# A Mamba gated RMS norm by one matmul on all partitions, with ln, exp and a Newton step, and a new schedule of the steps around it

## The chip, the cores and the metric

The kernel runs on one core of a Trainium2 chip. The metric is the device time of one execution in microseconds; the median of several runs counts. A core has five engines with queues of their own that synchronise by semaphores: PE (TensorE: matmuls, with its weight loads shown as PEld), DVE (VectorE), ACT (ScalarE), POOL (GpSimd) and SP (SyncE, here the issuer of most DMAs).

## The reference

A decoder trunk of two layers over 256 tokens of width 2048: a Mamba-2 mixer, then a block-sparse attention, each followed by a gated convolutional FFN and a post-norm. The change lies in the Mamba mixer alone:

```python
zxbcdt = x @ w_in
z, xbc, dt = ...
xbc = silu(causal_dwconv(xbc, conv_w, conv_b))
dt = softplus(dt + dt_bias)
a = -exp(a_log)
y = ssd_chunked(xs * dt[..., None], a * dt, b_ssm, c_ssm)
y = y + d_skip[:, None] * xs
y = y.reshape(Bsz, S, D_INNER) * silu(z)
yg = y.reshape(Bsz, S, N_SSM_GROUPS, D_INNER // N_SSM_GROUPS)
yg = yg * rsqrt(mean(square(yg), axis=-1, keepdims=True) + RMS_EPS)
y = yg.reshape(Bsz, S, D_INNER) * norm_w
return y @ w_out
```

There are 8 groups of 512 channels (8 heads of 64). The scan works in two chunks of 128 tokens; it needs the decays exp(acum[l] - acum[s]) within a chunk and exp(acum[l]) for the state that enters the second chunk. Everything is float32.

## The kernel before

All matrix products with weights run in split precision: a weight tile (128 partitions by 1024, 512 KB) is loaded by SP into `raw`, ScalarE makes its high part `hi` (L190), VectorE the low part `lo = raw - hi` (L191), and PE multiplies both with the split activations. One weight tile is one *step*. The body of the kernel is one loop over all steps: `products(i)` issues the matmuls of step i, and in the middle of a step `splits(i)` issues the split of the tile that is three steps ahead (four `hi` and four `lo` buffers, so a split has to wait until PE is done with the tile four before). After a step, `run(post, i)` issues whatever `at(i, f, ...)` has put there. So the order of each engine's queue is written out by hand, by step numbers; each engine works its queue strictly in that order, and dependences across engines become semaphore waits.

In the Mamba part, the columns of `w_in` for B, C and dt come first. Then follow the eight groups, each with eight steps of its x columns (`chX[g]`) and eight of its z columns (`chZ[g]`); `s0` is the first step of a group, so s0+16 is the next group's s0. In these steps the weights stand in PE and the activations stream. An even step multiplies first the high parts (L247: eight products with 512 columns) and then the low parts (L250: eight with 256 columns); an odd step the low parts first. The high products of an odd and the next even step thus stand side by side, and likewise the low ones.

Around these steps the group's own work is spread:

- `m_load` (s0+3): two POOL DMAs bring the cumulated decays of 8 heads, repeated over all partitions, into `mA` (one per chunk, two buffers).
- `m_decay` (s0+6 and s0+7, L717): eight ScalarE activations a chunk, `mA = relu(aux - mA)`; `m_exp` (s0+8, s0+9, L728): `exp(-mA)`.
- `m_into` (s0+7, L724): exponentials of the raw `mA` of the second chunk into `eA`, before its decays overwrite it.
- `m_cb` (s0+7): three PE products of B and C (L703, L704) into a PSUM tile, the masked `cb` by VectorE (L706) and a copy `bc` by ScalarE (L710).
- `Conv.gather` (L581, L582) and `Conv.taps` (ScalarE L604, VectorE L609) at s0+4 and s0+5 for one half of x, at s0+8 and s0+9 for the other; then Silu (L739), the masks (L732), transposes of `xc` (L748) into `xdt`, and the skip `y_d` (L757).
- after the z columns (next group's first steps): `y_off` and `y_diag` (PE L774, L765), then `z_gate` (s0+20), `z_square` (s0+21), `z_sum` (s0+22).
- `z_rms` (s0+23, L804): two PE products with one column each turn the sums of 128 partitions into one mean per token, tokens on partitions; VectorE adds epsilon (L806), POOL raises to the power -0.5 (L807).
- `z_diag` (s0+24, L813): two diagonals of these values. `z_scale` (s0+29, that is the next group's s0+13): a PE product of `ones` with the diagonals (L818) spreads them over all partitions, and VectorE scales `y` (L821). `z_split` (s0+30): the high and low part of `y` (L827, L828) for the output product. The last group's two run at s0+26 and s0+27, in the output projection.

PSUM tiles of these small products come from `tp_tile()` (two buffers); `xdt`, `y` and `sz` from four buffers of `t4k`.

Of the kernel before, what the change touches and what calls it, by code (L numbers as in the profile page):

```python
# [18 lines left out]
F32 = mybir.dt.float32  # L19
F32R = mybir.dt.float32r  # L20
AF = mybir.ActivationFunctionType
OP = mybir.AluOpType
AX = mybir.AxisListType

P = 128
D = 2048
S = 256
# [3 lines left out]
NG = 8  # L31
# [7 lines left out]
RMS_EPS = 1e-5  # L39
# [3 lines left out]
LINE = 64  # L43
# [48 lines left out]
def yoco_kernel(ctx: ExitStack, tc: tile.TileContext, x, lmg, lmb, lfg, lfb, x_t, columns, w, out):  # L92
    nc = tc.nc
    base = ctx.enter_context(tc.tile_pool(name="base", bufs=1))
# [12 lines left out]
    def tp_tile():  # L107
        return psum.tile([P, NC], F32, tag="tp", name="tp", bufs=2)


    ident = base.tile([P, P], F32, name="ident")
# [8 lines left out]
    def c1(name, j):  # L120
        i = COL_AT[name] + j
        return cols[:, i:i + 1]
# [201 lines left out]
    def at(i, f, *a):  # L324
        post.setdefault(i, []).append((f, a))
# [16 lines left out]
    bufs = {"h": base.tile([P, KD, 2, S], F32R, name="hT")}  # L342
# [146 lines left out]
    mhalf = base.tile([P, 2, 1], F32, name="mhalf")  # L489
# [32 lines left out]
    def open_pool(name):  # L522
        g = tc.tile_pool(name=name, bufs=1)
        pool[name] = (g, g.__enter__())
        return pool[name][1]
# [24 lines left out]
    ps = tp_tile()  # L550
# [7 lines left out]
    for p in range(2, 8):  # L558
# [3 lines left out]
    mp = open_pool("mamba")  # L562
# [4 lines left out]
    nc.gpsimd.memset(tri, 1.0)  # L567
    nc.gpsimd.affine_select(out=tri, in_=tri, compare_op=OP.is_ge, fill=0.0, base=0, pattern=[[1, P]],
                            channel_multiplier=-1)
    mean = base.tile([P, LINE], F32, name="mean")  # L570
    nc.gpsimd.memset(mean, 1.0 / NC)
    ones = base.tile([P, P], F32, name="ones")
    nc.gpsimd.memset(ones, 1.0)
    acum_d = dram.tile([NH, S], F32, name="acum_d")
    aux = mp.tile([P, 5, NH], F32, name="aux")

# [45 lines left out]
    def conv4(ch, j, dst, jd):  # L622

        return Conv(ch, j, dst, jd, [k * 48 for k in range(4)], "cw", "cb")
# [58 lines left out]
    G = [dict() for _ in range(NG)]  # L683
# [15 lines left out]
    def m_cb(g):  # L699
        ps = tp_tile()  # L700
        for c in range(2):
            sl = slice(c * P, (c + 1) * P)
            nc.tensor.matmul(ps[:, sl], BT[:, g, sl], CT[:, g, sl], start=True, stop=True)  # L703
        nc.tensor.matmul(ps[:, 2 * P:3 * P], BT[:, g, :P], CT[:, g, P:], start=True, stop=True)  # L704
        cb = mp.tile([P, 2, P], F32, tag="cb", name="cb", bufs=1)
        nc.vector.tensor_mul(cb, ps[:, :2 * P].rearrange("p (c l) -> p c l", c=2),  # L706
                             tri.unsqueeze(1).to_broadcast([P, 2, P]))

        bc = mp.tile([P, P], F32, tag="bc", name="bc", bufs=1)
        nc.scalar.copy(bc, ps[:, 2 * P:3 * P])  # L710
        G[g]["cb"], G[g]["bc"] = cb, bc

    def m_decay(g, c):

# [2 lines left out]
            nc.scalar.activation(t[:, h, :], t[:, h, :], AF.Relu, scale=-1.0, bias=aux[:, 2 + c, 8 * g + h:8 * g + h + 1])  # L717

    def m_into(g):

        G[g]["eA"] = e = mp.tile([P, 4, P], F32, tag="eA", name="eA", bufs=1)
        for q in range(2):
            ps = slice(64 * q, 64 * q + 64)
            nc.scalar.activation(e[ps], G[g]["A", 1][ps].rearrange("p (j q) l -> p j q l", q=2)[:, :, q, :], AF.Exp)  # L724

    def m_exp(g, c):
        t = G[g]["A", c]
# [6 lines left out]
    def x_new(g):  # L734
        G[g]["xc"] = mp.tile([P, 4, S], F32, tag="xc", name="xc")
        return G[g]["xc"]
# [62 lines left out]

    def z_rms(g):  # L800

        ps = tp_tile()
        for h in range(2):
            nc.tensor.matmul(ps[:, h:h + 1], G[g]["sz"][:, 0, h * P:(h + 1) * P], mean[:, :1], start=True, stop=True)  # L804
        rr = mp.tile([P, 2, 1], F32, tag="rr", name="rr")
        nc.vector.tensor_scalar(rr[:, :, 0], ps[:, :2], RMS_EPS, None, op0=OP.add)  # L806
        nc.gpsimd.tensor_tensor(rr, rr, mhalf, op=OP.pow)  # L807
        G[g]["rr"] = rr

    def z_diag(g):  # L810
        G[g]["rd"] = rd = mp.tile([P, 2, P], F32, tag="rd", name="rd", bufs=1)
        for h in range(2):
            nc.vector.tensor_scalar(rd[:, h], ident, G[g]["rr"][:, h, :], None, op0=OP.mult)  # L813

    def z_scale(g):

        ps = tp_tile()
        nc.tensor.matmul(ps[:, :S], ones, G[g]["rd"].rearrange("p h t -> p (h t)"), start=True, stop=True)  # L818
        y = G[g]["y"]
        for i in range(4):  # L820
            nc.vector.scalar_tensor_tensor(y[:, i, :], y[:, i, :], c1("nw", 4 * g + i), ps[:, :S], op0=OP.mult,  # L821
                                           op1=OP.mult)

    def z_split(g):
        y = G[g]["y"]
# [11 lines left out]
    for g in range(NG):  # L837
        s0 = chX[g].first
        at(s0 + 3, m_load, g)
        at(s0 + 7, m_cb, g)  # L840
        at(s0 + 7, m_into, g)
        at(s0 + 6, m_decay, g, 0)
        at(s0 + 7, m_decay, g, 1)
        at(s0 + 8, m_exp, g, 0)
        at(s0 + 9, m_exp, g, 1)
        conv4(chX[g], 4 * g, lambda g=g: x_new(g), 0).plan()
        at(s0 + 11, x_silu, g)
        at(s0 + 11, m_mask, g, 0)
        at(s0 + 12, m_mask, g, 1)
        if g:  # L850
            at(s0 + 13, z_scale, g - 1)
            at(s0 + 14, z_split, g - 1)
        at(s0 + 13, x_turn, g)
        at(s0 + 13, y_d, g)
        for b in range(2):
            at(chZ[g].ready(b), z_gather, g, b)
            at(chZ[g].ready(b) + 1, z_silu, g, b)
        at(s0 + 18, y_off, g)
        at(s0 + 18, y_diag, g)
        at(s0 + 20, z_gate, g)  # L860
        at(s0 + 21, z_square, g)
        at(s0 + 22, z_sum, g)
        at(s0 + 23, z_rms, g)
        at(s0 + 24, z_diag, g)
    at(s0 + 26, z_scale, NG - 1)
    at(s0 + 27, z_split, NG - 1)


    def chain(norm, nxt=None, after=None):
# [133 lines left out]
    A = {}  # L1003
# [76 lines left out]
    for h in range(HEADS):  # L1080
        i, j = divmod(h, 4)
# [87 lines left out]
```

## Time and profile before

| what | us |
|---|---|
| median of 3 runs (2553.05 to 2553.3) | 2553.09 |
| the profiled execution's own time | 2553.77 |
| its span, first to last instruction | 2552.0 |
| PE busy in the span | 2534.4 |
| VectorE busy | 1648.0 |
| ScalarE busy | 1351.8 |
| POOL busy | 71.7 |

A timeline row has the start in us from the span's beginning, its length, the engine, the line of the kernel, operation, what is written and read, shapes and the count of instructions merged into it; in brackets the idle time before it and what ended that. Lengths overlap: neighbours in one queue are pipelined, so the distance between two starts is the better price. A group row ends with busy us and mean ns of one, then the idle us before them. A float32 matmul that is not in split form appears as two or more records.

### The profile page before, as it was taken

Reading aid. Unit: us, or ns where it says so; the run is one execution under the profiler, and the core shown is the slowest. Engines: PE = TensorE matmul, PEld = TensorE weight load, DVE = VectorE, ACT = ScalarE, POOL = GpSimd, SP = SyncE. Lnnn points to the kernel's source line nnn. Section 1 sums busy time; section 2 is a strip of 40 time slices with the busy share of each in tenths; the row PEclk is TensorE's granted clock in tenths of the full one; section 3 lists DMA queues with packets and bytes.
Section 4 is the critical chain, followed back from the end, with each engine's and each line's share of the span. In section 5 each row is a group of like instructions: output and inputs, shape, how many; then the busy total and the mean of one; then the engine's idle time right before and its main releaser. Section 6 shows DMA issues by size and latency. Waiting matters only on the chain.

```text
span 2552.0 us, 36102 instructions
## 1 busy us (share of the span) xinstructions
PE 2534.4 (99%) x14031; PEld 2202.9 (86%) x14031; DVE 1648.0 (65%) x2122; ACT 1351.8 (53%) x1761; POOL 71.7 (3%) x89
## 2 busy tenths in 40 slices
PE   9999999999999999999999999999999999999998
PEld 8888888888888888888888888888888888888887
DVE  6768777854676766666444645655767666665545
ACT  6677677733455555555334444543555555554333
POOL 0000000000200000000000200000200000000001
PEclk9999999999999999999999999999999999999999
DMA  7655655557565555655666655456655555556564
GB/s 257 204 168 190 199 190 173 190 198 234 184 225 190 184 196 182 198 185 195 202 226 201 221 189 174 158 172 229 217 192 191 189 190 189 185 195 205 198 223 165
DMA packets 141499, 501.02 MB, mean 196 GB/s; under 512 B 15616, under 2 KB 16128, under 8 KB 141328
## 3 DMA queue, kind: packets, MB, share of 16 engines
q1 hardware_dynamic: 136976, 483.45, 57.3%
q0 software_dynamic: 4064, 14.75, 1.7%
q8 instruction: 110, 1.80, 0.3%
q14 instruction: 61, 0.50, 0.1%
q10 hardware_dynamic: 288, 0.52, 0.1%
HBM read 490.20 MB, written 8.45 MB: 195 GB/s over the span
## 4 chain that ended last, share of the span: by engine, by line
PE 93%; ACT 3%; DVE 2%; issue 1%; DMA 0%; SPq 0%; DVEq 0%; ACTq 0%
PE acc L247 37%; PE acc L250 20%; PE acc L218 11%; PE acc L214 11%; PE acc L213 11%; DVE lo L191 1%; ACT hi L190 1%; ACT mA L717 1%; DVE xc L609 1%; PE acc L765 1%; PE tp L218 0%; PE tp L214 0%; PE tp L213 0%; ACT L724 0%; ACT eA L724 0%
## 5 line engine op out<-in xcount | busy, mean ns | idle before, releaser
L191 DVE TENSOR_TENSOR lo<-raw,hi 128x1024 fp32r<-128x1024 f32 (+1 forms) x871 | 1062.7, 1225 | 791.1 <-ACT hi L190 656.1
L190 ACT CAST hi<-raw 128x1024 fp32r<-128x1024 f32 (+1 forms) x871 | 911.9, 1048 | 847.7 <-PE acc L218 372.9
L247 PE MATMUL acc<-hT,hi 128*128 128x512 f32 x4496 | 1062.2, 391 | 1.6 <-ACT hi L190 1.4
L247 PEld LDWEIGHTS acc<-hT,hi 128*128 128x128 f32 x4496 | 830.8, 188 | 166.9 <-ACT hi L190 2.6
L250 PEld LDWEIGHTS acc<-hT,lo 128*128 128x128 f32 x4496 | 565.3, 191 | 21.1 <-DVE lo L191 5.2
L250 PE MATMUL acc<-hT,lo 128*128 128x256 f32 x4496 | 575.0, 283 | 3.6 <-DVE lo L191 3.6
L214 PE MATMUL acc<-lo,gT 128*128 128x512 f32 (+1 forms) x678 | 254.5, 378 | 0.0
L213 PE MATMUL acc<-hi,gT 128*128 128x512 f32 (+1 forms) x678 | 254.1, 377 | 0.0
L218 PE MATMUL acc<-hi,gT 128*128 128x512 f32 (+1 forms) x678 | 200.7, 377 | 0.0
L214 PEld LDWEIGHTS acc<-lo,gT 128*128 128x128 f32 x678 | 127.7, 188 | 23.3
L213 PEld LDWEIGHTS acc<-hi,gT 128*128 128x128 f32 x678 | 127.5, 188 | 23.1
L218 PEld LDWEIGHTS acc<-hi,gT 128*128 128x128 f32 x678 | 124.8, 188 | 23.7
L213 PE MATMUL acc<-hi,yT 128*128 128x512 f32 (+1 forms) x270 | 98.8, 370 | 0.0
L214 PE MATMUL acc<-lo,yT 128*128 128x512 f32 (+1 forms) x270 | 98.6, 369 | 0.0
L213 PE MATMUL acc<-hi,hT 128*128 128x512 f32 x192 | 78.8, 410 | 0.0
L218 PE MATMUL acc<-hi,yT 128*128 128x512 f32 (+1 forms) x270 | 77.7, 369 | 0.0
L214 PE MATMUL acc<-lo,hT 128*128 128x512 f32 x192 | 75.4, 393 | 0.0
L609 DVE SCALAR_TENSOR_TENSOR g<-u,cols,g 128x254 f32<-128x254 f32 (+1 forms) x176 | 73.3, 478 | 2.9 <-ACT g L604 2.8
L582 DVE TENSOR_TENSOR u<-u,acc 128x512 f32<-128x512 f32 x108 | 73.3, 680 | 0.8 <-ACT u L581 0.8
L609 DVE SCALAR_TENSOR_TENSOR v<-u,cols,v 128x254 f32<-128x254 f32 (+1 forms) x176 | 73.0, 477 | 0.0
L984 ACT CAST gT<-v 128x512 fp32r<-128x512 f32 x44 | 27.3, 621 | 84.5 <-DVE v L983 84.5
L581 ACT COPY u<-acc 128x512 f32<-128x512 f32 x108 | 62.1, 576 | 0.0
(206 smaller groups left out, 1818.6 us busy)
## 6 DMA issues: line engine op xcount, KB each, us to landing
raw<-in_w SPq DMA_DIRECT2D x881, 512.0 KB, 3.5
mA<-acum_d POOLq DMA_DIRECT2D x16, 512.0 KB, 6.2
hres<-r POOLq DMA_DIRECT2D x12, 512.0 KB, 6.7
r<-hres SPq DMA_DIRECT2D x12, 512.0 KB, 4.6
r<-in_x SPq DMA_DIRECT2D x4, 512.0 KB, 5.6
gb<-in_ln_mix_g SPq DMA_DIRECT2D x8, 256.0 KB, 5.2
gb<-in_ln_mix_b SPq DMA_DIRECT2D x8, 256.0 KB, 6.0
gb<-in_ln_ffn_g SPq DMA_DIRECT2D x8, 256.0 KB, 5.3
```

The lines of the kernel that those rows point to most:

```text
L190: nc.scalar.copy(h[:, sl], t[:, sl])
L191: nc.vector.tensor_sub(l[:, sl], t[:, sl], h[:, sl].bitcast(F32))
L213: nc.tensor.matmul(a, th, h[:, kk, sl], start=k == 0, stop=False)
L214: nc.tensor.matmul(a, th, l[:, kk, sl], start=False, stop=False)
L218: nc.tensor.matmul(a, ch.x.lo(k)[:, ts], h[:, kk, sl], start=False, stop=k == ch.nk - 1)
L247: nc.tensor.matmul(banks[j], w[:, kk, js], ch.x.both(k), start=begins, stop=ends, skip_group_check=True)
L250: nc.tensor.matmul(banks[j][:, :S], w[:, kk, js], ch.x.hi(k), start=begins, stop=ends, skip_group_check=True)
L581: nc.scalar.copy(dst, p[:, :, S:])
L582: nc.vector.tensor_add(dst, dst, p[:, :, :S])
L609: nc.vector.scalar_tensor_tensor(d, u[:, i % 2, :S - k], c1(self.at_w, w[n - 1 - k] + self.ia + i), d, op0=OP.mult, op1=OP.add)
L717: nc.scalar.activation(t[:, h, :], t[:, h, :], AF.Relu, scale=-1.0, bias=aux[:, 2 + c, 8 * g + h:8 * g + h + 1])
L984: nc.scalar.copy(h, v[:, sl])
```

## The change

- `z_rms` becomes one product of a 128x128 matrix of 1/512 with the 256 columns of sums, so that the mean square stands on all partitions; VectorE adds epsilon while it copies from PSUM into a free part of `sz`. The power -0.5 is made by ScalarE as exp(-0.5 ln v) (`z_log`, `z_root`) and improved by a Newton step on VectorE (`z_newton`, three operations). `z_diag`, the POOL power and the product with `ones` go; `z_scale` reads the result from SBUF.
- Gate, square and sums come one step sooner (s0+19 to s0+21). Scaling and splitting come at s0+27 and s0+28 in all groups.
- `eA` is no longer made from `mA`: two POOL DMAs bring the same values into `eA` at s0+3, right behind `m_load`, and one exponential over all partitions runs at s0+10.
- The decays come one step sooner (s0+5, s0+6), the exponentials one later (s0+9, s0+10); the copy `bc` is taken out of `m_cb` and put at s0+9.

```diff
-    mean = base.tile([P, LINE], F32, name="mean")
+    mean = base.tile([P, P], F32, name="mean")
     nc.gpsimd.memset(mean, 1.0 / NC)
-    ones = base.tile([P, P], F32, name="ones")
-    nc.gpsimd.memset(ones, 1.0)
...
-        bc = mp.tile([P, P], F32, tag="bc", name="bc", bufs=1)
-        nc.scalar.copy(bc, ps[:, 2 * P:3 * P])
-        G[g]["cb"], G[g]["bc"] = cb, bc
+        G[g]["cb"], G[g]["bc"] = cb, ps[:, 2 * P:3 * P]
+
+    def m_bc(g):
+        bc = mp.tile([P, P], F32, tag="bc", name="bc", bufs=1)
+        nc.scalar.copy(bc, G[g]["bc"])
+        G[g]["bc"] = bc
...
         G[g]["eA"] = e = mp.tile([P, 4, P], F32, tag="eA", name="eA", bufs=1)
+        s = acum_d[8 * g:8 * g + 8, P:]
         for q in range(2):
-            ps = slice(64 * q, 64 * q + 64)
-            nc.scalar.activation(e[ps], G[g]["A", 1][ps].rearrange("p (j q) l -> p j q l", q=2)[:, :, q, :], AF.Exp)
+            nc.gpsimd.dma_start(e[64 * q:64 * q + 64], bass.AP(tensor=s.tensor, offset=s.offset + q * S,
+                                                               ap=[[0, 64], [2 * S, 4], [1, P]]))
+
+    def m_into_exp(g):
+        nc.scalar.activation(G[g]["eA"], G[g]["eA"], AF.Exp)
...
-        ps = tp_tile()
-        for h in range(2):
-            nc.tensor.matmul(ps[:, h:h + 1], G[g]["sz"][:, 0, h * P:(h + 1) * P], mean[:, :1], start=True, stop=True)
-        rr = mp.tile([P, 2, 1], F32, tag="rr", name="rr")
-        nc.vector.tensor_scalar(rr[:, :, 0], ps[:, :2], RMS_EPS, None, op0=OP.add)
-        nc.gpsimd.tensor_tensor(rr, rr, mhalf, op=OP.pow)
-        G[g]["rr"] = rr
-
-    def z_diag(g):
-        G[g]["rd"] = rd = mp.tile([P, 2, P], F32, tag="rd", name="rd", bufs=1)
-        for h in range(2):
-            nc.vector.tensor_scalar(rd[:, h], ident, G[g]["rr"][:, h, :], None, op0=OP.mult)
+        G[g]["ms"] = ps = tp_tile()[:, :S]
+        nc.tensor.matmul(ps, mean, G[g]["sz"][:, 0, :], start=True, stop=True)
+        nc.vector.tensor_scalar(G[g]["sz"][:, 1, :], ps, RMS_EPS, None, op0=OP.add)
+
+    def z_log(g):
+        nc.scalar.activation(G[g]["sz"][:, 2, :], G[g]["sz"][:, 1, :], AF.Ln)
+
+    def z_root(g):
+        r = G[g]["sz"][:, 2, :]
+        nc.scalar.activation(r, r, AF.Exp, scale=-0.5)
+
+    def z_newton(g):
+        v, r, t = (G[g]["sz"][:, i, :] for i in (1, 2, 3))
+        nc.vector.tensor_mul(t, r, r)
+        nc.vector.scalar_tensor_tensor(t, t, -0.5, v, op0=OP.mult, op1=OP.mult)
+        nc.vector.scalar_tensor_tensor(r, t, 1.5, r, op0=OP.add, op1=OP.mult)
 
     def z_scale(g):
-        ps = tp_tile()
-        nc.tensor.matmul(ps[:, :S], ones, G[g]["rd"].rearrange("p h t -> p (h t)"), start=True, stop=True)
-        y = G[g]["y"]
+        y, r = G[g]["y"], G[g]["sz"][:, 2, :]
         for i in range(4):
-            nc.vector.scalar_tensor_tensor(y[:, i, :], y[:, i, :], c1("nw", 4 * g + i), ps[:, :S], op0=OP.mult,
-                                           op1=OP.mult)
+            nc.vector.scalar_tensor_tensor(y[:, i, :], y[:, i, :], c1("nw", 4 * g + i), r, op0=OP.mult, op1=OP.mult)
...
         at(s0 + 3, m_load, g)
+        at(s0 + 3, m_into, g)
         at(s0 + 7, m_cb, g)
-        at(s0 + 7, m_into, g)
-        at(s0 + 6, m_decay, g, 0)
-        at(s0 + 7, m_decay, g, 1)
-        at(s0 + 8, m_exp, g, 0)
-        at(s0 + 9, m_exp, g, 1)
+        at(s0 + 9, m_bc, g)
+        at(s0 + 5, m_decay, g, 0)
+        at(s0 + 6, m_decay, g, 1)
+        at(s0 + 9, m_exp, g, 0)
+        at(s0 + 10, m_exp, g, 1)
+        at(s0 + 10, m_into_exp, g)
...
-        if g:
-            at(s0 + 13, z_scale, g - 1)
-            at(s0 + 14, z_split, g - 1)
...
-        at(s0 + 20, z_gate, g)
-        at(s0 + 21, z_square, g)
-        at(s0 + 22, z_sum, g)
+        at(s0 + 19, z_gate, g)
+        at(s0 + 20, z_square, g)
+        at(s0 + 21, z_sum, g)
         at(s0 + 23, z_rms, g)
-        at(s0 + 24, z_diag, g)
-    at(s0 + 26, z_scale, NG - 1)
-    at(s0 + 27, z_split, NG - 1)
+        at(s0 + 24, z_log, g)
+        at(s0 + 25, z_root, g)
+        at(s0 + 26, z_newton, g)
+        at(s0 + 27, z_scale, g)
+        at(s0 + 28, z_split, g)
```

## The prediction

> **What bounds the kernel now.** I read the page's busy shares first, then its clock row and its chain that ended last.
>
> ```profile
> span 2552.0 us, 36102 instructions
> PE 2534.4 (99%) x14031; PEld 2202.9 (86%) x14031; DVE 1648.0 (65%) x2122; ACT 1351.8 (53%) x1761; POOL 71.7 (3%) x89
> PEclk9999999999999999999999999999999999999999
> PE 93%; ACT 3%; DVE 2%; issue 1%; DMA 0%; SPq 0%; DVEq 0%; ACTq 0%
> ```
>
> TensorE sets the time, at full clock. An edit on another engine is therefore worth only the time for which PE waits because of it, plus whatever matmul time it adds or removes. Next comes the view of waits, cut to the Mamba groups (120 to 560 us): who PE waits for there, and the longest wait that ScalarE has in the edited lines. Columns: total us, times, longest.
>
> ```profile
> PE acc L250 <- DVE lo L191: 3.6, 8, 0.5
> ACT bc L710 <- DVE cb L706: 21.6, 8, 2.8
> ```
>
> PE waits exactly eight times, once per group, for VectorE's low part of a weight tile. The timeline of PE in group 1 shows where, and group 0 serves as a control, since no earlier group's RMS work (L804, L818) falls into it.
>
> ```profile
> 171.29 2.08 PE L250 MATMUL acc<-hT,lo 128*128 128x256 f32 x16
> 173.20 2.00 PE L247 MATMUL acc<-hT,hi 128*128 128x512 f32 x8
> 175.04 0.50 PE L804 MATMUL tp<-mean,sz 128*128 128x1 f32 x4
> ...
> 176.07 2.10 PE L247 MATMUL acc<-hT,hi 128*128 128x512 f32 x8
> ...
> 189.14 1.11 PE L250 MATMUL acc<-hT,lo 128*128 128x256 f32 x8
> 190.69 1.22 PE L250 MATMUL acc<-hT,lo 128*128 128x256 f32 x8 [0.44 <-DVE lo L191]
> 191.75 2.01 PE L247 MATMUL acc<-hT,hi 128*128 128x512 f32 x8
> 193.59 0.60 PE L818 MATMUL tp<-rd,ones 128*128 128x256 f32 x2
> ...
> 196.74 2.08 PE L250 MATMUL acc<-hT,lo 128*128 128x256 f32 x16
> ```
>
> ```profile
> 123.32 2.00 PE L247 MATMUL acc<-hT,hi 128*128 128x512 f32 x8
> ...
> 125.75 2.10 PE L247 MATMUL acc<-hT,hi 128*128 128x512 f32 x8
> ...
> 141.49 2.01 PE L247 MATMUL acc<-hT,hi 128*128 128x512 f32 x8
> ...
> 146.06 2.08 PE L250 MATMUL acc<-hT,lo 128*128 128x256 f32 x16
> ```
>
> Sixteen L250 products take 173.20 - 171.29 = 1.91 us undisturbed. The sixteen around the wait take 191.75 - 189.14 = 2.61. The stall thus costs **0.70 us** a group; the 0.44 of the label counts only from the modelled end of the product before. It falls ahead of the low products of step 13 (steps counted from a group's first, s0; odd steps begin with the low part).
>
> Why that tile is late is read on ScalarE and VectorE:
>
> ```profile
> 164.15 1.05 ACT L190 CAST hi<-raw 128x1024 fp32r<-128x1024 f32 x1 [5.67 <-PE acc L247]
> ...
> 176.81 0.27 ACT L710 COPY bc<-tp 128x128 f32<-128x128 f32 x1 [2.74 <-DVE cb L706]
> 177.10 1.28 ACT L724 ACT_TABLE_LOAD   x1
> 178.39 1.28 ACT L724 ACTIVATE eA<-mA 64x512 f32<-64x512 f32 x2
> 179.70 2.45 ACT L717 ACTIVATE mA<-mA,aux 128x128 f32<-128x128 f32 x8
> 182.06 1.03 ACT L190 CAST hi<-raw 128x1024 fp32r<-128x1024 f32 x1
> 183.00 1.06 ACT L728 ACTIVATE mA<-mA 128x1024 f32<-128x1024 f32 x1
> ...
> 186.33 1.08 ACT L604 ACTIVATE xc<-u,cols 128x256 f32<-128x256 f32 x2
> 187.31 1.99 ACT L190 CAST hi<-raw 128x1024 fp32r<-128x1024 f32 x2
> ```
>
> ```profile
> 186.95 2.55 DVE L609 SCALAR_TENSOR_TENSOR xc<-u,cols,xc 128x255 f32<-128x255 f32 x6 [0.23 <-ACT xc L604]
> 189.42 2.35 DVE L191 TENSOR_TENSOR lo<-raw,hi 128x1024 fp32r<-128x1024 f32 x2
> ...
> 196.92 1.65 DVE L821 SCALAR_TENSOR_TENSOR y<-y,cols,tp 128x256 f32<-128x256 f32 x4
> ```
>
> ScalarE stands idle for 2.74 us behind `bc`, which needs a product that PE makes only at the end of step 7. Then a table load, two exponentials and eight decays run in one block, so the filter taps start at 186.33, VectorE's taps at 186.95, and step 13's low part ends at 189.42 + 1.22 = 190.64. PE wanted it at 189.14 + 0.96 = 190.10.
>
> **The change, part by part.** PE first. L804 is two one-column products, and L818 a 256-column one; both go, and one 256-column product in the place of L804 comes. From the same block to the same block, group 1 takes 176.07 - 173.20 = 2.87 where group 0, without L804, takes 125.75 - 123.32 = 2.43, so L804 costs 0.44. Around L818, 196.74 - 191.75 = 4.99 against 146.06 - 141.49 = 4.57: 0.42. The new product is of L818's shape, and so 0.42 too; bounds 0.24 (its two passes at the pace of L250's 256 columns, 1.91 / 16 each) and 0.60 (L818's whole row). Removed minus added: 0.44 + 0.42 - 0.42 = 0.44, over 8 groups **-3.5 us**, between -2.1 and -5.0.
>
> Then the stall. I lay out ScalarE's queue in the new order from the split at 164.15, whose start PE fixes in both kernels. Each item is taken at the distance to the next start in the rows above: split 0.96, 1024-wide activation 0.96, eight decays 2.36, table 1.29, taps 0.98, `bc` 0.29, and the copy of `u` 0.48 (its row below, less the 0.1 by which neighbours overlap, 1.06 against 0.96). Items that no row shows are Ln and the power's Exp at 128x256; the nearest is the attention's exponential of that size:
>
> ```profile
> L1048 ACT ACTIVATE s<-s,mx 128x256 f32<-128x256 f32 x16 | 8.0, 498 | 0.0
> L787 ACT ACTIVATE sz<-sz 128x512 f32<-128x512 f32 x16 | 10.1, 634 | 12.8 <-DVE sz L582 12.7
> L581 ACT COPY u<-acc 128x512 f32<-128x512 f32 x108 | 62.1, 576 | 0.0
> L798 DVE TENSOR_TENSOR sz<-sz 128x256 f32<-128x256 f32 x8 | 3.4, 425 | 0.3
> mA<-acum_d POOLq DMA_DIRECT2D x16, 512.0 KB, 6.2
> ```
>
> I take 0.50 (bounds 0.30, one of the eight 128-wide decays, and 0.63, the 512-wide row). Square, pulled a step forward, and copy of `u`: 1.44. Split, decays of chunk 0, taps, split, decays of chunk 1, two splits: 0.96 + 2.36 + 0.98 + 0.96 + 2.36 + 1.92 = 9.54. Table, Ln, copy of `u`, split: 3.23. Table, Exp, `bc`, exponential of chunk 0: 3.04. With the first split's 0.96 that is 18.21 us, so the second taps start at 182.36 instead of 186.33. VectorE's taps follow 0.62 later (186.95 - 186.33), take 2.47, and the low part 1.22: step 13's tile is ready at 186.67, **3.4 us before** PE wants it. Ln at 0.63 and Exp at 0.63 would take 0.3 of that. The stall's place is covered: 8 x 0.70 = **-5.6 us**. What pays for it is the idle 2.74 us, filled by decays, and one eA exponential in place of two and behind the tile.
>
> What could be late next: step 15's low part. Between the two tiles VectorE now has the Newton step (three operations of L798's width, 0.43 each and some hundredths between dependent ones: 1.4), step 14's tile 1.22, the scaling 1.65 and a mask of the tile's width 1.22. From 186.67 that gives 192.2, and the tile is done at 193.4; PE reaches it at 196.74 + 0.96 - 0.70 - 0.42 = 196.6. The transposes of `xc` wait for Silu, which ends after a further exponential 0.96, eA 0.54, split 0.96, table 1.29 and Silu 1.06 past 184.3: at 189.1, against 193.59 - 0.70 = 192.9. Both have over 3 us. Even Newton at 0.7 an operation would leave 2.5. The other VectorE edit puts one addition of L798's width in place of three smaller operations. A window over group 1 shows that there is room (columns: busy us of PE, its loads, VectorE, ScalarE, POOL):
>
> ```profile
> 149.80:200.50 50.70, 50.26 (x318) 44.41 (x317) 36.50 (x51) 36.48 (x56) 2.49 (x3) 1.00 0.57 188
> 160.76 1.76 POOL L697 DMA_DIRECT2D mA<-acum_d  x2 [68.27 <-DVE y L778]
> ```
>
> VectorE is busy 36.50 of 50.70 us, ScalarE 36.48; they get at most 1.4 + 0.4 and 1.29 + 1.0 - 0.65 us more. A group's two eA transfers queue on POOL behind its two mA ones and ahead of nothing of that group, since the power has left POOL; two issues of 0.88 after 162.5 and 6.2 us to land end near 170.5, and eA is read near 185.3. The first decays, a step earlier, want mA at 167.5; it lands at 160.76 + 6.2 = 167.0. That cover is thin, but a wait of a few tenths is taken from the 3.4 us. Weights come on SP's queue, which nothing new enters. Two buffers are held longer: the PSUM one with `bc`'s product by two steps, which the next but one user wants only a group later, and `sz` to the scaling at s0+27, whose next writer, the next group's `xdt` at s0+29, stands behind the scaling on the same VectorE.
>
> The last group's split moves a step later in the output projection; a step there is twelve 512-column products at (193.59 - 191.75) / 8 = 0.23 us, 2.76.
>
> ```profile
> 541.45 1.23 DVE L828 TENSOR_TENSOR yT<-y,yT 128x1024 fp32r<-128x1024 f32 x1
> 546.65 0.39 PE L213 MATMUL acc<-hi,yT 128*128 128x512 f32 x1
> ```
>
> Its low part then ends at 542.68 + 2.76 = 545.4. PE first reads those columns' high part at 546.65 - 0.42 = 546.2 and the low part four products later, so this stays hidden.
>
> One price speaks against the change. The row at 177.10 starts 0.02 us after `bc` ends and the exponential follows at 178.39: a switch of tables costs 1.29 here, and the new queue has three a group (Ln, Exp, Silu) instead of two. The Trainium skill, "ScalarE: Activation LUTs", section "What ACT_TABLE_LOAD costs", counts a drain of about 1.38 us on top of each load, 2.66 in all. The trace shows no such gap, so the sum keeps 1.29.
>
> Sum: -3.5 - 5.6 = **-9.1 us**. Against the profiled execution's 2553.77 (span 2552.0 and 1.8 around it) this gives 2544.7 (span 2542.9); that execution lay 0.7 above the median of 2553.09, so the median becomes **2544.0**.
>
> **The rivals.**
> 1. *The stall stays, or moves by one tile.* For it: ScalarE and VectorE each get more work in the same stage. Against: over 3 us of slack at each place worked out. Only the PE term remains: 2553.1 - 3.5 = 2549.6.
> 2. *Each table switch empties ScalarE first.* Were a switch to cost the load twice, 1.29 more, step 13's tile would be 2.6 us later and still in time, but Silu would end 3.9 later, at 193.0 against 192.9, and the transposes would hold PE 0.1 us a group: 2544.0 + 0.8 = 2544.8. Against: the gapless rows. By the drain that the Trainium skill's "ScalarE: Activation LUTs" states it would be 0.3 us a group and 2546.4.
> 3. *Slower: the decays wait for mA.* They now stand one step earlier in ScalarE's queue, ahead of the splits of steps 9 to 13, and 16 more transfers share POOL's queue. Stalls begin once mA lands 0.5 + 3.4 = 4 us later than now, that is 10.2 us after issue, and the gain is gone at 11.5. At twice today's 6.2, 12.4 us, each of seven groups (the first has its data long before) loses 2.2 us, 15 in all: 2559. Against: eA is queued behind mA, and a quarter of its size.
>
> **How the numbers follow.** Forecast 0.82, rival 1 0.07, rival 2 0.05, rival 3 0.06. The forecast's own range is 2542.5 (PE term at -5.0) to 2547.5 (PE term at -2.1 and of each stall only the labelled 0.44, 3.5 in all). Rival 2 lies inside it; 2542.3 to 2548.0 holds a little over 8 in 10. A measurement of this kernel tells about 0.2%, 5.1 us, from no change. Forecast and rival 2 are faster than that (0.87), rival 1 is within it (0.07), rival 3 beyond it on the other side (0.06).
>
> **What would show it.** Right: no wait of PE for `lo` in any group, group period 50.7 - 0.70 - 0.44 = 49.55 us, `bc` without idle time before it, three table loads a group at 1.28 with nothing ahead. Wrong: a new PE wait after `xc` transposes (rival 2), idle time before the first decay ended by a DMA (rival 3), or the same L250 wait (rival 1).

## The result, and the profile after

| | before | changed |
|---|---|---|
| median of 6 runs, us | 2553.20 (2552.93 to 2553.72) | **2544.41** (2543.70 to 2545.19) |
| profiled execution, us | 2553.77 | 2545.19 |
| its span, us | 2552.0 | 2542.8 |
| PE waiting for `lo` in the Mamba groups | 8 times | never |
| period of a group, mean product to mean product, us | 50.68 | 49.55 |

The ratio of changed to before is 0.9966 with a 95% interval of 0.9953 to 0.9979: 8.8 us gained, where 9.1 were forecast (2544.0).

The page of the changed kernel:

```profile
span 2542.8 us, 36109 instructions
PE 2529.3 (99%) x13999; PEld 2199.4 (86%) x13999; DVE 1657.0 (65%) x2130; ACT 1362.4 (54%) x1779; POOL 75.8 (3%) x96
PE 97%; DVE 1%; DMA 0%; issue 0%; ACT 0%; SPq 0%; DVEq 0%
```

VectorE, ScalarE and POOL have more to do than before, PE has 32 products fewer, and PE's share of the chain that ended last has gone from 93% to 97%: the links through VectorE and ScalarE have left the chain. The view of waits of the changed kernel, PE's alone and over the whole span (total us, times, longest):

```profile
PE tp L552 <- POOL ident masks.py:199: 1.4, 1, 1.4
PE acc L247 <- ACT hi L190: 0.7, 2, 0.5
PE acc L218 <- DVE hT L381: 0.6, 3, 0.2
...
```

The row `L250 <- DVE lo` is gone (the two rows left out are smaller and of other lines), and cut to 120 to 560 us the view is empty: no wait has taken its place. The timeline of PE in group 1, the counterpart of the one in the prediction (line 808 is the new mean product; start, length, and the rest as before):

```profile
171.84 2.01 PE L247 MATMUL acc<-hT,hi 128*128 128x512 f32 x8
173.68 0.60 PE L808 MATMUL tp<-sz,mean 128*128 128x256 f32 x2
...
174.70 2.10 PE L247 MATMUL acc<-hT,hi 128*128 128x512 f32 x8
...
187.76 2.08 PE L250 MATMUL acc<-hT,lo 128*128 128x256 f32 x16
189.68 2.01 PE L247 MATMUL acc<-hT,hi 128*128 128x512 f32 x8
...
199.80 2.08 PE L250 MATMUL acc<-hT,lo 128*128 128x256 f32 x16
...
223.23 0.60 PE L808 MATMUL tp<-sz,mean 128*128 128x256 f32 x2
```

The sixteen low products, eight of step 12 and then eight of step 13, now run in one row and take 189.68 - 187.76 = 1.92 us instead of 2.61. From block to block across the mean product it is 174.70 - 171.84 = 2.86; group 0 of before, without one, had 2.43, so the new product costs 0.43. The next group's mean product comes at 223.23, 49.55 us later.

Two windows show that the time came from there. Before, from the first group's product of C and B to the last group's mean product:

```profile
125.16:529.36 404.20, 400.64 (x2491) 352.80 (x2490) 303.42 (x402) 287.77 (x436) 17.56 (x21) 1.00 0.57 185
```

The same stretch of the changed kernel:

```profile
124.56:520.05 395.49, 395.49 (x2463) 349.22 (x2462) 311.37 (x409) 291.65 (x441) 21.21 (x28) 1.00 0.60 195
```

The columns are the length, busy us of PE, its loads, VectorE, ScalarE and POOL, then the granted clock. The stretch is 8.71 us shorter. Before, PE was idle in it for 404.20 - 400.64 = 3.56 us; now it is busy from end to end. The other 5.15 us are busy time: seven times 0.43 of products, 3.0, and about 2.1 that are the rest of the stalls, which the labels of the waits don't count (8 x (0.70 - 0.44)). Ahead of this stretch the changed kernel is 0.6 us earlier; it is so already in the first 13 us (a row of products that began at 12.99 begins at 12.38), ahead of every edited step. Behind the stretch it takes 0.1 us longer.

ScalarE's queue in group 1 of the changed kernel:

```profile
166.11 2.46 ACT L718 ACTIVATE mA<-mA,aux 128x128 f32<-128x128 f32 x8
...
175.46 1.28 ACT L812 ACT_TABLE_LOAD   x1 [0.49 <-DVE sz L809]
176.75 0.42 ACT L812 ACTIVATE sz<-sz 128x256 f32<-128x256 f32 x1
...
180.23 0.25 ACT L711 COPY bc<-tp 128x128 f32<-128x128 f32 x1
...
181.34 1.08 ACT L602 ACTIVATE xc<-u,cols 128x256 f32<-128x256 f32 x2
...
184.22 0.62 ACT L729 ACTIVATE eA<-eA 128x512 f32<-128x512 f32 x1
...
185.79 1.28 ACT L744 ACT_TABLE_LOAD   x1
```

VectorE's queue behind it, in the changed kernel:

```profile
181.96 2.55 DVE L607 SCALAR_TENSOR_TENSOR xc<-u,cols,xc 128x255 f32<-128x255 f32 x6 [2.11 <-ACT xc L602]
184.42 1.22 DVE L191 TENSOR_TENSOR lo<-raw,hi 128x1024 fp32r<-128x1024 f32 x1
...
190.67 1.22 DVE L191 TENSOR_TENSOR lo<-raw,hi 128x1024 fp32r<-128x1024 f32 x1
...
197.61 3.49 DVE L191 TENSOR_TENSOR lo<-raw,hi 128x1024 fp32r<-128x1024 f32 x3
```

`bc` (L711) has no idle time ahead of it any more; the 2.74 us are gone. The taps follow at 181.34, and step 13's tile is ready at 184.42 + 1.22 = 185.64. PE wants it behind step 12's eight products, at 187.76 + 0.96 = 188.72: 3.1 us of slack. Of the three splits that begin at 197.61, the first is the tile of step 17 (step 1 of the next group). It is done at 198.83, and PE wants it at 199.80 + 0.96 = 200.76: **1.9 us, the narrowest place among the group's low parts**. The prediction did not work it out.

### The profile page after: what moved, and what is told of

It reads as the page before. It is cut to its first block, busy times and chain, and to the rows that moved or that the text cites. A ratio compares the mean times of both kernels' runs of the same rounds, so it can differ in the third digit from the quotient of the medians.

```text
span 2542.8 us, 36109 instructions
## 1 busy us (share of the span) xinstructions
PE 2529.3 (99%) x13999; PEld 2199.4 (86%) x13999; DVE 1657.0 (65%) x2130; ACT 1362.4 (54%) x1779; POOL 75.8 (3%) x96
## 4 chain that ended last, share of the span: by engine, by line
PE 97%; DVE 1%; DMA 0%; issue 0%; ACT 0%; SPq 0%; DVEq 0%
PE acc L247 40%; PE acc L250 21%; PE acc L218 11%; PE acc L214 11%; PE acc L213 11%; PE acc L770 1%; DMA raw<-in_w 0%; PE tp L218 0%; PE tp L214 0%; DVE lo L191 0%; PE tp L213 0%; PE tp L779 0%; PE acc L753 0%; PE tp L1042 0%; DVE r L445 0%
## 5 line engine op out<-in xcount | busy, mean ns | idle before, releaser
L250 PEld LDWEIGHTS acc<-hT,lo 128*128 128x128 f32 x4496 | 564.8, 191 | 15.9 <-issue 1.2
L250 PE MATMUL acc<-hT,lo 128*128 128x256 f32 x4496 | 572.9, 283 | 0.0
L438 POOL TENSOR_TENSOR rs<-rs,mhalf 128x1 f32<-128x1 f32 x8 | 7.4, 931 | 2003.0 <-DVE nb L439 2003.0
```

The lines of the kernel that those rows point to most:

```text
L250: nc.tensor.matmul(banks[j][:, :S], w[:, kk, js], ch.x.hi(k), start=begins, stop=ends, skip_group_check=True)
L438: nc.gpsimd.tensor_tensor(self.rs[:, h, :], self.rs[:, h, :], mhalf[:, 0, :], op=OP.pow)
```

## The experiments

The forecast rests on two terms and on a ledger of slack. The theory to be tested: the terms are independent; the stall ends because `bc` no longer stands idle at the head of ScalarE's queue; the products are worth 0.44 us a group; the rest of the change is worth nothing in itself. The main competitor: the gain is one knot of the sooner gate, the decays and the shorter chain together, and its parts alone would do little. Times are medians; the kernel before, beside these runs, took 2552.7 to 2552.9.

| experiment | us | ratio to before (95%) | group period, us |
|---|---|---|---|
| schedule without the new mean-square chain | 2547.21 | 0.9978 (0.9969 to 0.9987) | 49.98 |
| before, with only `bc` moved | 2547.33 | 0.9978 (0.9969 to 0.9987) | 49.99 |
| before, with only the new chain | 2582.15 | 1.0114 (1.0099 to 1.0130) | 54.84 |
| changed, gate, squares, sums one step later | 2555.37 | 1.0010 (1.0001 to 1.0019) | 51.09 |
| changed, mean product twice | 2547.51 | 0.9980 (0.9971 to 0.9989) | 49.96 |
| changed, `eA` made on ScalarE | 2545.67 | 0.9972 (0.9961 to 0.9983) | 49.78 |
| changed, four more ScalarE operations | 2550.39 | 0.9990 (0.9981 to 1.0000) | 50.29 |
| changed, nine more | 2577.86 | 1.0099 (1.0082 to 1.0116) | 53.73 (group 1; others 53.62 to 54.06) |
| changed, mean product in one pass | **2542.69** | 0.9960 (0.9947 to 0.9972) | 49.23 |
| changed, decays at their old steps | 2544.34 | 0.9966 (0.9953 to 0.9979) | 49.55 |

### The schedule alone

The changed kernel with the old mean product, POOL power, diagonal and product with `ones` at their old steps; decays, exponentials, `bc`, `eA`, gate, squares and sums stay at the new ones.

```diff
...
+        if g:
+            at(s0 + 13, z_scale, g - 1)
+            at(s0 + 14, z_split, g - 1)
...
-        at(s0 + 24, z_log, g)
-        at(s0 + 25, z_root, g)
-        at(s0 + 26, z_newton, g)
-        at(s0 + 27, z_scale, g)
-        at(s0 + 28, z_split, g)
+        at(s0 + 24, z_diag, g)
+    at(s0 + 26, z_scale, NG - 1)
+    at(s0 + 27, z_split, NG - 1)
```

> The new schedule (decays, bc, eA by DMA, gate, squares and sums) with the old mean, power and spreading product. My theory: the two terms are independent, so this takes the 0.70 us stall of each group (-5.6 us, about 2547.6, group period 49.98) and leaves the 0.44 us of matmul time. Rival (the stall went because the RMS work left the crowded steps): the wait of PE for lo before step 13's low products stays and the time is within 1 us of before.

Measured: 2547.21, which is 5.7 us below before, and no wait of PE in any group. The new chain is worth the rest: 49.98 - 49.55 = 0.43 us a group, 2.8 us in the medians. Eight times 0.43 would be 3.4; the medians also hold what differs outside the groups, and the profiled execution of the schedule alone is 0.5 us earlier than the changed kernel's within the first 12 us. By the periods the two terms add up.

### One copy moved, nothing else

```diff
+        G[g]["cb"], G[g]["bc"] = cb, ps[:, 2 * P:3 * P]
+
+    def m_bc(g):

         bc = mp.tile([P, P], F32, tag="bc", name="bc", bufs=1)
-        nc.scalar.copy(bc, ps[:, 2 * P:3 * P])
-        G[g]["cb"], G[g]["bc"] = cb, bc
+        nc.scalar.copy(bc, G[g]["bc"])
+        G[g]["bc"] = bc
...
         at(s0 + 9, m_exp, g, 1)
+        at(s0 + 9, m_bc, g)
```

> The kernel before with one edit: the copy bc moved from step s0+7 to s0+9. My theory: ScalarE's idle 2.74 us behind bc alone made step 13's tile 0.54 us late; without it the tile is some 2.5 us early, no PE wait, -5.6 us, about 2547.6, period 49.98. Rival (the block of decays, table load and exponentials is the cause, whatever stands before it): the PE wait stays at 0.4 us or more, time as before.

Measured: 2547.33, 0.1 us from the whole schedule. VectorE's and PE's rows of this kernel:

```profile
184.95 2.36 DVE L191 TENSOR_TENSOR lo<-raw,hi 128x1024 fp32r<-128x1024 f32 x2
```

```profile
187.52 2.08 PE L250 MATMUL acc<-hT,lo 128*128 128x256 f32 x16
```

Step 13's tile is ready at 184.95 + 1.22 = 186.17 and wanted at 187.52 + 0.96 = 188.48, 2.3 us early, and the sixteen low products of steps 12 and 13 run in one row. The place of a 0.25 us copy in ScalarE's queue was thus the whole cause of the stall. The idea of one knot falls.

### The new chain alone

Before, with the new product, Ln, Exp, Newton step and scaling at the new steps s0+23 to s0+28; everything else, `bc` included, stays where it was.

```diff
...
-        if g:
-            at(s0 + 13, z_scale, g - 1)
-            at(s0 + 14, z_split, g - 1)
...
-        at(s0 + 24, z_diag, g)
-    at(s0 + 26, z_scale, NG - 1)
-    at(s0 + 27, z_split, NG - 1)
+        at(s0 + 24, z_log, g)
+        at(s0 + 25, z_root, g)
+        at(s0 + 26, z_newton, g)
+        at(s0 + 27, z_scale, g)
+        at(s0 + 28, z_split, g)
```

> The kernel before with the new RMS chain alone (one product, ln, exp, Newton, scaling at s0+27), decays, bc, eA and gate as before. My theory: two more table loads' worth of ScalarE work (Ln, Exp, one more load each: 2.3 to 3.6 us) meets a queue that is already 0.54 us late at step 13, so PE waits 2 to 5 us a group: 2553 + 8 x (2 to 5) - 3.5 = 2566 to 2590. Rival (the RMS chain is what pays): 2553 - 3.5 - up to 5.6 = 2544 to 2550.

Measured: 2582.15, slower than before by 29 us. PE's waits of this kernel:

```profile
PE acc L250 <- DVE lo L191: 22.5, 14, 2.4
PE acc L247 <- ACT hi L190: 8.5, 8, 1.2
```

ScalarE's rows in group 1 of this kernel:

```profile
175.35 0.27 ACT L708 COPY bc<-tp 128x128 f32<-128x128 f32 x1 [2.74 <-DVE cb L704]
175.63 1.28 ACT L722 ACT_TABLE_LOAD   x1
...
181.65 1.28 ACT L805 ACT_TABLE_LOAD   x1
```

The idle 2.74 us before `bc` is still there, and behind it two more table loads a group, with Ln and Exp, enter a queue that had already cost PE 0.70 us a group (there are four now, at 175.63, 181.65, 183.38 and 191.57). The splits are behind them, and PE waits for high and low parts, 4.16 us a group (54.84 - 50.68). So the 0.44 us of products can't be had by the chain alone: the terms add up when the schedule comes first, and do not in the other order. Whether `bc` moved alone would be schedule enough for the chain was not tried.

### Gate, squares and sums back to their old steps

```diff
-        at(s0 + 19, z_gate, g)
-        at(s0 + 20, z_square, g)
-        at(s0 + 21, z_sum, g)
+        at(s0 + 20, z_gate, g)
+        at(s0 + 21, z_square, g)
+        at(s0 + 22, z_sum, g)
```

> The changed kernel with gate, squares and sums back at s0+20 to s0+22. The prediction gave the sooner gate no price. Theory: the squares would then stand behind chunk 0's decays or the taps on ScalarE and the sums behind the taps on VectorE, so the mean product's input is late and PE waits in front of it, some 1.5 us a group: about 2556. Rival: the sums have a step of slack as in the kernel before, no change, 2544.

Measured: 2555.37, 11 us above the changed kernel, more than its whole gain. The wait of PE that is new in this kernel:

```profile
PE tp L808 <- DVE sz L803: 9.2, 7, 1.3
```

And the timeline in front of it:

```profile
166.16 1.06 ACT L798 ACTIVATE sz<-y 128x1024 f32<-128x1024 f32 x1 [0.72 <-DVE y L795]
...
169.47 1.08 ACT L602 ACTIVATE xc<-u,cols 128x256 f32<-128x256 f32 x2
170.09 2.55 DVE L607 SCALAR_TENSOR_TENSOR xc<-u,cols,xc 128x255 f32<-128x255 f32 x6 [2.29 <-ACT xc L602]
...
173.69 0.68 DVE L802 TENSOR_TENSOR sz<-sz 128x512 f32<-128x512 f32 x1
...
174.98 0.67 PE L808 MATMUL tp<-sz,mean 128*128 128x256 f32 x2 [1.31 <-DVE sz L803]
```

The square waits for the gate; the eight decays stand between it and the taps on ScalarE; VectorE's taps wait 2.29 us for these, the sums stand behind the taps, and PE stands before the mean product: 51.09 - 49.55 = 1.54 us a group, seven times. The prediction gave this edit no price at all. It is a condition: next to the decays of s0+5 the sums must be early. With the old chain, late sums do no harm beside late decays (the kernel with only `bc` moved has both, and no wait); whether they would do with the new chain and late decays was not tried.

### The mean product twice

```diff
         nc.tensor.matmul(ps, mean, G[g]["sz"][:, 0, :], start=True, stop=True)
+        nc.tensor.matmul(ps, mean, G[g]["sz"][:, 0, :], start=True, stop=True)
```

> The changed kernel with the mean product issued twice in each group (the second overwrites the first with the same values). Theory: PE is the bound and the product stands in its stream at its full 0.42 us, so +0.42 x 8 = +3.4 us, about 2547.8, group period 49.55 + 0.42 to 0.44 = 49.98. Rival (the product hides beside weight loads or waits): period 49.55, 2544.4.

Measured: 2547.51, 3.1 us more; the two products start 0.44 us apart in the trace, and the period grows by 0.41. A 256-column float32 product of this kind costs about what the prediction took, 0.42, and nothing covers it.

### `eA` made by ScalarE again

No DMAs for `eA`; two exponentials of `mA` at s0+6, ahead of chunk 1's decays.

```diff
...
-        at(s0 + 3, m_into, g)
...
         at(s0 + 5, m_decay, g, 0)
+        at(s0 + 6, m_into, g)
         at(s0 + 6, m_decay, g, 1)
...
-        at(s0 + 10, m_into_exp, g)
```

> The changed kernel with eA made again by two ScalarE exponentials of mA (at s0+6, ahead of chunk 1's decays) in place of the DMAs. Theory: a fourth table load (1.29) and 1.28 of exponentials stand ahead of step 13's tile, 2.6 of the 3.1 us of slack that the changed kernel shows there (ready 185.64, wanted 188.72): no wait at step 13, at most 0.3 us a group where the backlog reaches the next group's step 1: 2544.4 to 2547. Rival (the DMA detour is what pays): the wait at step 13 is back, 0.5 us or more a group, 2548 or more.

Measured: 2545.67, 1.3 us more, and 0.23 us more in the period. PE's rows of this kernel show where:

```profile
199.75 2.31 PE L250 MATMUL acc<-hT,lo 128*128 128x256 f32 x16
201.90 3.82 PE L247 MATMUL acc<-hT,hi 128*128 128x512 f32 x16
```

The second eight are the low products of step 17, and the sixteen take 2.15 us instead of 1.92, too little for the waits to name it. The fourth table load and the two exponentials take 2.60 us of ScalarE's queue (170.46 to 173.06 in its timeline) where the one exponential took 0.52, so the queue is 2.1 us later, 0.2 more than the 1.9 us of slack there. This was the first sign that the narrow place is step 17.

### Four more operations, and nine more

To measure the slack: `n` activations (Relu, 128x512, on a tile of zeros that nothing reads) at s0+9, ahead of the exponential of chunk 0.

```diff
...
+    def m_more(g):
+        for _ in range(4):
+            nc.scalar.activation(idle, idle, AF.Relu)
...
+        at(s0 + 9, m_more, g)
         at(s0 + 9, m_exp, g, 0)
```

> The changed kernel with four further ScalarE activations (128x512 on a tile of zeros, 0.54 us each from start to start) at s0+9 ahead of chunk 0's exponential. Theory: 2.15 us is within the 3.1 us of slack at step 13: no PE wait, 2544.4. Rival (the queues have no real slack, the stall is only just gone): PE waits about 2 us a group, 2560.

> The same with nine further activations, 4.86 us. Theory: 1.8 us more than the slack, so PE waits 1.8 us in front of step 13's low products, 8 x 1.8 = 14 us, about 2559; up to 2566 if the backlog reaches the next group's step 1 as well. Rival (a slack much larger than worked out): no wait, 2544.4.

Four: 2550.39, so the expectation of no wait missed. ScalarE's rows, then PE's, of the kernel with four:

```profile
179.95 2.63 ACT L719 ACTIVATE idle<-idle 128x512 f32<-128x512 f32 x4
182.48 1.04 ACT L740 ACTIVATE mA<-mA 128x1024 f32<-128x1024 f32 x1
```

```profile
199.37 1.11 PE L250 MATMUL acc<-hT,lo 128*128 128x256 f32 x8
200.97 1.22 PE L250 MATMUL acc<-hT,lo 128*128 128x256 f32 x8 [0.48 <-DVE lo L191]
202.03 3.82 PE L247 MATMUL acc<-hT,hi 128*128 128x512 f32 x16
```

The four cost 182.48 - 179.95 = 2.53 us and not 2.15. A likely reason is that each reads the tile that the one before writes; no run here separates that from others. Step 13 is not touched, as its 3.1 us say. The wait is at step 17 again: 202.03 - 199.37 = 2.66 instead of 1.92, which is 0.74 a group, near 2.53 - 1.9 = 0.6.

Nine: 2577.86, beyond the 2559 to 2566 that were expected. ScalarE is later by 5.86 us in the trace (the exponential at 187.67 against the row of nine at 181.81), and PE in the kernel with nine:

```profile
189.20 1.11 PE L250 MATMUL acc<-hT,lo 128*128 128x256 f32 x8
192.98 2.07 PE L250 MATMUL acc<-hT,lo 128*128 128x256 f32 x8 [2.66 <-DVE lo L191]
```

Now the wait is at step 13, ahead of the second half of its sixteen low products: PE wants the tile at 189.20 + 0.96 = 190.16 and starts at 192.98, 2.8 us later, and 5.86 - 3.08 = 2.78. The slack at step 13 is thus confirmed to a tenth. Yet all waits for `lo` make 21.1 us by their labels, and the kernel lost 33.4 (32.2 between the spans of the profiled executions, 2575.0 and 2542.8). The expectation had no term for the rest; the last section says where it is.

### The product in one pass

The mean product of the changed kernel has two records, which are read here as two passes over its 256 float32 columns. Here the sums are written in the split's format fp32r, and so is the matrix of 1/512, and the product runs once.

```diff
+    meanr = base.tile([P, P], F32R, name="meanr")
+    nc.vector.tensor_copy(meanr, mean)
...
-        nc.vector.tensor_add(sz[:, 0], sz[:, 0], sz[:, 1])
+        G[g]["sr"] = sr = mp.tile([P, S], F32R, tag="sr", name="sr", bufs=1)
+        nc.vector.tensor_add(sr, sz[:, 0], sz[:, 1])
...
-        nc.tensor.matmul(ps, mean, G[g]["sz"][:, 0, :], start=True, stop=True)
+        nc.tensor.matmul(ps, meanr, G[g]["sr"], start=True, stop=True)
```

> The changed kernel with the sums of squares rounded to fp32r, so that the mean product runs in one pass instead of two. Theory: 256 columns in one pass cost 0.12 us (the L250 rows) against 0.42 to 0.44, so 0.2 to 0.3 us a group, -1.6 to -2.6 us, about 2542.3, group period 49.25 to 49.35. Rival: its weight load is not hidden, nothing gained, 49.55.

Measured: 2542.69 (2541.89 to 2542.83), 1.7 us below the changed kernel and so the fastest kernel of this case. PE's rows of it:

```profile
174.18 0.28 PE L811 MATMUL tp<-sr,meanr 128*128 128x256 f32 x1
...
223.41 0.28 PE L811 MATMUL tp<-sr,meanr 128*128 128x256 f32 x1
```

One record instead of two, and a period of 223.41 - 174.18 = 49.23, 0.32 less. (Eight times 0.32 would be 2.6; in its profiled execution the first mean product of all comes 0.5 us later than the changed kernel's, 174.18 against 173.68, ahead of any gain.) About three quarters of the product's 0.43 us could still be had, because PE is where the time is.

### The decays at their old steps

```diff
-        at(s0 + 5, m_decay, g, 0)
-        at(s0 + 6, m_decay, g, 1)
+        at(s0 + 6, m_decay, g, 0)
+        at(s0 + 7, m_decay, g, 1)
```

> The changed kernel with the decays back at s0+6 and s0+7. Theory: their sooner place is not needed once bc stands at s0+9; ScalarE's order shifts and step 13's tile comes about 1 us later, still 2 us before PE wants it: 2544.4, no wait. Rival (the sooner decays are what made the room): the L250 wait returns, 2548 or more.

Measured: 2544.34, the changed kernel's time, with its period and no wait in a group. The sooner decays, which the ledger of the prediction used to fill the idle time before `bc`, are not needed.

## Why the prediction was right

**What bounds the kernel.** PE, by its waits and its products alone: the window before had 3.56 us of idle PE, the one after none, and what lies outside the groups changed by 0.6 us ahead of them and by 0.1 in all behind them.

**The PE term**, -3.5 (0.44 a group). Right: 0.43 by the period between the schedule alone and the changed kernel. The new product's price, borrowed from line 818, held to 0.02 (0.43 by its block, 0.41 to 0.44 by doubling it).

**The stall**, -5.6 (0.70 a group). Right in size, 0.69 by the period when `bc` alone moves, and right to be taken from the sixteen products and not from the label.

**Its cause.** The idle 2.74 us behind `bc`, and the block that followed it. Shown, and narrower than it was put: "What pays for it is the idle 2.74 us, filled by decays, and one eA exponential in place of two and behind the tile". Moving the copy was enough. `eA` by DMA is worth about 1.3 us by itself, at another place, and the decays nothing.

**The ledger of step 13**, 3.4 us of slack. Measured 3.1, and confirmed by nine added operations. The item that it left out is the 0.49 us in which Ln's load waits for the addition on VectorE; the two splits ahead of that took 0.3 more than the 1.92 in the sum, and Ln and Exp at 0.42, with a `bc` of 0.25, were cheaper than the prices taken.

**"What could be late next."** Incomplete. Step 15's tile had 191.89 against 194.24 + 0.96, 3.3 us (3.2 forecast), and the transposes 3.4 (3.8 forecast). The narrowest place, step 17 with 1.9 us, was not among them. That changed no number, but the sentence "Even Newton at 0.7 an operation would leave 2.5" spoke of the wrong place, and with four more operations the loss came there.

**Sooner gate, squares and sums.** The prediction placed the square in ScalarE's queue and went no further. Without this edit the rest of the change gives no gain at all (2555.37). Here the prediction was lucky: the forecast was right because the edit is in the change, not because its use was seen.

**Rival 1**, the stall stays or moves: refuted, by waits that are empty.

**Rival 2**, a switch of tables empties ScalarE. The groups of table loads of the changed kernel between 120 and 560 us (busy us and mean ns of one, then idle us ahead):

```profile
L744 ACT ACT_TABLE_LOAD x8 | 10.3, 1283 | 0.1
L812 ACT ACT_TABLE_LOAD x8 | 10.3, 1283 | 3.4 <-DVE sz L809 3.4
L817 ACT ACT_TABLE_LOAD x8 | 10.3, 1283 | 0.1
```

Three loads a group, as forecast, 1283 ns each, and eight of them together have 0.1 us of idle time ahead; the 3.4 us at line 812 is VectorE's addition. The activation follows within 0.01 us (175.46 + 1.28 against 176.75). The Trainium skill, "ScalarE: Activation LUTs", section "What ACT_TABLE_LOAD costs", has the 1283 ns right; its drain of about 1.38 us does not appear at any of these 24 loads, and the trace decides.

**Rival 3**, the decays wait for `mA`. The transfers of the changed kernel (KB each, median us from issue to landing):

```profile
mA<-acum_d POOLq DMA_DIRECT2D x16, 512.0 KB, 5.8
...
eA<-acum_d POOLq DMA_DIRECT2D x16, 128.0 KB, 6.6
```

The 16 more transfers did not slow `mA` (6.2 before). In group 1 it landed at 164.1, 2.0 us ahead of the decays at 166.11; the prediction had 0.5. `eA` landed by 167.4 and is read at 184.22.

**The sum**, 9.1 forecast and 8.8 measured. The stretch of the two windows holds eight stalls and seven of the eight products, 5.6 + 3.0 by the measured terms, and gave 8.71. That the total came within 0.3 us of the forecast is in part luck: three things of about 0.6 us each that are not in the sum partly offset one another. They are the 0.6 us gained before any edited step, about as much that is lost behind the groups (where the eighth product's 0.43 should have been gained, the stretch is 0.1 longer), and 2.4 us around the profiled execution's span instead of 1.8. The span fell by 9.2.

## What to carry to other kernels

When the bounding engine waits for a tile, follow the late queue back to the first instruction that stands idle at its head: here a 0.25 us copy, queued 2.7 us before its operand existed, held up everything behind it, and moving it alone gave two thirds of the gain. Write the ledger of slack for every tile up to the end of the repeating stage, not for the two nearest ones; the narrowest place was four steps behind the repaired stall. And price an edit that only moves work sooner by working out what would stand in front of it if it were left: it may be the condition on which the rest of the change depends.

## What the hardware showed that was not expected

Waits of 2.4 to 2.7 us can cost more than themselves. In the kernel with nine added operations, windows around the waits for `lo` (length, busy us of the engines, granted clock, DMA share and GB/s):

```profile
137.00:146.00 9.00, 7.37 (x45) 6.33 (x44) 7.89 (x11) 8.97 (x12) 0.00 (x0) 1.00 0.37 117
190.00:198.00 8.00, 5.34 (x28) 4.63 (x26) 7.93 (x16) 7.39 (x9) 0.00 (x0) 0.79 0.39 132
193.00:194.00 1.00, 1.00 (x5) 1.00 (x6) 0.93 (x3) 0.98 (x2) 0.00 (x0) 0.50 0.17 33
...
405.00:415.00 10.00, 7.33 (x47) 6.39 (x46) 9.86 (x18) 9.39 (x12) 0.00 (x0) 1.00 0.31 107
```

In group 1 the granted clock falls to 0.50, and its mean over 8 us is 0.79: 8 x 0.21 = 1.7 us of clock lost, or 3.4 us at half speed. Not all of it costs PE time, since some lies within the wait. The price is read from the periods. The group with the wait at 405 us waited as long, its clock stayed at 1.00, and its period is 53.62; less its further wait of 0.88 and the 0.26 that a label leaves out, that is 52.48. Group 1 has 53.73 and so lost 1.25 us. The clock fell in six of the seven groups with a wait of 2.65 to 2.67 us, and they lost 1.25 to 1.6 each, 8.8 together; after the waits of 1.63 (at 137 us) and 0.88 it stayed at 1.00. That accounts for the 32.2 us between the spans: 21.1 by the labels, some 2.3 that the nine labels leave out (0.26 each, the 0.70 - 0.44 of before), and 8.8.

The kernel with the new chain alone had seven waits of 2.40 to 2.42 us, each some 3 us behind one of 1.2. After six of them the clock stayed at 1.00; after the last, which ended at 521.72, it fell too:

```profile
524.00:526.00 2.00, 2.00 (x6) 1.41 (x6) 2.00 (x6) 0.32 (x1) 0.00 (x0) 0.50 0.65 213
```

A wait of 2.4 us thus cost the clock in one case of seven, one of 2.7 in six of seven. The Trainium skill, "TensorE: Matmul & The Clock Gate", Part 1, tells of a free-running window of about 3.4 us, of which an idle one halves the clock. The length of the slow stretches, and that waits of one length sometimes cost the clock and sometimes not, agree with it; that a wait of 2.4 to 2.7 us is enough is less than it states.

Two one-column float32 products cost as much as one of 256 columns: 0.44 us for the old mean, 0.43 for the new one, which leaves its result on all partitions besides. And activations that rewrite one 128x512 tile start 0.63 us apart (2.53 / 4), where `eA`'s, of the same width and followed by a split of another tile, leaves 0.52 to the next start (184.22 to 184.74).
